# Attention with the scores turned round: keys on the partitions, queries along the free dimension

## The chip, the cores and the metric

The kernel runs on one core of a Trainium2 chip. The metric is the device time of one execution in microseconds (us). TensorE (PE) multiplies, VectorE (DVE) and ScalarE (ACT) work element by element, GpSimd (POOL) does small vector work, and SyncE (SP) issues the transfers.

## The reference

A two-layer trunk: a gated linear recurrence (HGRN2), then multi-head latent attention (MLA), for 1024 latent tokens that see 256 context tokens. The change is in the attention of the second layer: 16 heads, 1024 queries, 1280 keys.

```python
def _attend(q_nope, q_pe, k_nope, k_pe, v):
    s = (jnp.einsum('bqhd,bkhd->bhqk', q_nope, k_nope, preferred_element_type=jnp.float32)
         + jnp.einsum('bqhr,bkr->bhqk', q_pe, k_pe, preferred_element_type=jnp.float32))
    p = jax.nn.softmax(s * MLA_SCALE, axis=-1)
    return jnp.einsum('bhqk,bkhd->bqhd', p.astype(v.dtype), v)
```

## The kernel before

Everything is float32. A product that needs float32 precision is made of three float32r products (`mm3`): each operand is split into a high part, which ScalarE rounds, and a low part, which VectorE subtracts (`split`: `hi` and `lo`, in the tiles `wh`/`wl`, `ph`/`pl`, `oh`/`ol`).

The keys are not expanded per head. `attn_prep` folds a head's key weight into its queries (`qah`, `qal`, in buffers of the tags `wl` and `wh`), so all heads share one latent key matrix (`kh`, `kl`, 128 by 1280), one rope matrix `kr` and one value matrix (`vh`, `vl`, ten tiles of 128 keys). A head's own value weight (`wvh`, `wvl`) is applied behind the average.

The work goes in tiles of 128 queries, 8 to a head, 128 in all. Below, a *unit* is two tiles (256 queries of one head); there are 64 units.

- `attn_scores`, for one tile: queries on the partitions, keys along the free dimension, in blocks of 512, 512 and 256. Five products a block (lines 855 to 859) fill a PSUM tile `s`, of which there are four. VectorE reduces each block to a maximum per query (line 861) and the three to one (867). ScalarE takes the exponential with that maximum as bias and gives the sum of the row (871). VectorE divides the 128 by 1280 probabilities `pr` by the sum (877, 878, 882).
- `attn_values`, for a unit: TensorE transposes the probabilities, 20 blocks of 128 by 128 (902), into PSUM tiles `pt`. ScalarE and VectorE split each pair of key tiles out of PSUM (907, recorded at 214 and 215) into `ph` and `pl`, and 30 products sum the values in `pv` (915). The average is split (920 to 922, the low part on GpSimd), multiplied by the head's value weight (925), by the gate `z` (927), and stored.
- `attend` sorts the steps of these generators by a due time; TensorE keeps this order, while the other engines are ordered by the scheduler. `attn_prep` of the next head runs in between. Behind the last unit the first eight steps of the output projection (`lead`, called `tail` in `attend`) are mixed in.

Of the kernel before, what the change touches and what calls it, by code (L numbers as in the profile page):

```python
# [18 lines left out]
P = 128  # L19
# [18 lines left out]
class Net:  # L38
# [631 lines left out]
    def mla_in(self, pool, pp, kp, a, hh, hl, st):  # L670
# [6 lines left out]
        for c in range(NT):  # L677
# [39 lines left out]
            )  # L717
            if lat:
# [64 lines left out]
    def attn_prep(self, pool, pp, a, st, qrD, zT, h, box):  # L783
# [4 lines left out]
        z = t(pool, [P, LQ], F32, f"za{h % 2}")  # L788
        nc.sync.dma_start(z, zT[h])
# [7 lines left out]
        self.split(wvh, wvl, wv)  # L797
        ps = t(pp, [P, 512], F32, G_TAG)
# [6 lines left out]
        self.split(wqh, wql, ps[:, : 2 * P].rearrange("p (a b) -> p a b", a=2), SCALE)  # L805
        yield
        if h % 2 == 0:
            par = h // 2 % 2
            if ("low", par) not in box:
                box["low", par] = [t(pool, [P, LQ], F32R, f"qrl{par}") for _ in range(2)]  # L810
                for rl in box["low", par]:
                    nc.vector.memset(v32(rl[64:]), 0.0)
            box["pair"] = [(t(pool, [P, LQ], F32R, f"qrh{par}"), rl) for rl in box["low", par]]
            for b, n in self.qgs:
                sl = slice(b * P, (b + n) * P)
                ps = t(pp, [P, 512], F32, G_TAG)
                for j in range(n):
                    nc.tensor.transpose(ps[:, j * P : (j + 1) * P], qr[:, b + j], self.ident)
                for i, (rh, rl) in enumerate(box["pair"]):
                    own, twin = (slice(0, 64), slice(64, P))[:: 1 - 2 * i]  # L820
                    src = ps[own, : n * P]
                    nc.scalar.activation(rh[own, sl], src, AF.Copy, scale=SCALE)
                    nc.vector.scalar_tensor_tensor(
                        rl[:64, sl], src, SCALE, v32(rh[own, sl]), ALU.mult, ALU.subtract
                    )
                    TWIN(nc)(rh[twin, sl], rh[own, sl])
                yield
        qah = t(self.wpool, [P, LQ], F32R, "wl")
        qal = t(self.wpool, [P, LQ], F32R, "wh")
        for b, n in self.qgs:  # L830
            sl = slice(b * P, (b + n) * P)
            ps = t(pp, [P, 512], F32, G_TAG)
            for k in range(2):
                self.mm3(ps[:, : n * P], wqh[:, k], wql[:, k], st["qh"][:, k, sl], st["ql"][:, k, sl], k == 0, k == 1)
            self.split(qah[:, sl], qal[:, sl], ps[:, : n * P])
            yield
        box[h] = (qah, qal) + box["pair"][h % 2] + (wvh, wvl, z)

    def attn_scores(self, pool, pp, st, box, i, prs):
        nc, t, NT = self.nc, self.t, self.NT  # L840
        mm = nc.tensor.matmul
        LK = NT * P
        blocks = [(o, min(512, LK - o)) for o in range(0, LK, 512)]
        nb = len(blocks)
        h, j = divmod(i, self.NL)
        qah, qal, rh, rl = box[h][:4]
        js = slice(j * P, (j + 1) * P)
        mx = t(pool, [P, 4], F32, "mx")
        sm = t(pool, [P, 4], F32, "sm")
        pr = t(pool, [P, LK], F32, "pr")  # L850
        sc = []
        for b, (o, w) in enumerate(blocks):
            s = t(pp, [P, 512], F32, "s")
            ks = slice(o, o + w)
            mm(s[:, :w], qah[:, js], st["kh"][:, ks], start=True, stop=False)  # L855
            mm(s[:, :w], qah[:, js], st["kl"][:, ks], start=False, stop=False)  # L856
            mm(s[:, :w], qal[:, js], st["kh"][:, ks], start=False, stop=False)  # L857
            mm(s[:, :w], rh[:, js], st["kr"][:, ks], start=False, stop=False)  # L858
            mm(s[:, :w], rl[:, js], st["kr"][:, ks], start=False, stop=True)  # L859
            with self.tc.high_priority(offset=AT_PRIO):  # L860
                nc.vector.tensor_reduce(mx[:, b : b + 1], s[:, :w], AX.X, ALU.min)  # L861
            sc.append(s)
            if b < nb - 1:
                yield
        nm = t(pool, [P, 1], F32, "nm")
        with self.tc.high_priority(offset=AT_PRIO):
            nc.vector.tensor_reduce(nm, mx[:, :nb], AX.X, ALU.min)  # L867
        for b, (o, w) in enumerate(blocks):
            yield
            with self.tc.high_priority(offset=EXP_PRIO):  # L870
                nc.scalar.activation(  # L871
                    pr[:, o : o + w], sc[b][:, :w], AF.Exp, bias=nm, scale=-1.0,
                    accum_out=sm[:, b : b + 1],
                )
        yield
        rs = t(pool, [P, 1], F32, "rs")
        nc.vector.tensor_reduce(rs, sm[:, :nb], AX.X, ALU.add)
        nc.vector.reciprocal(rs, rs)
        if i % NORM_ACT[1] < NORM_ACT[0]:
            nc.scalar.activation(pr, pr, AF.Copy, scale=rs)  # L880
        else:
            nc.vector.tensor_scalar(pr, pr, rs, None, ALU.mult)
        prs[i] = pr

    def attn_values(self, pool, pp, st, box, u, prs, yT):
        nc, t, NT = self.nc, self.t, self.NT
        tiles = [i for i in (2 * u, 2 * u + 1) if i < self.NH * self.NL]
        h, b = divmod(tiles[0], self.NL)
        n = len(tiles)
        N = n * P  # L890
        wvh, wvl, z = box[h][4:]
        np_ = -(-NT // 2)
        parts = {}
        acc = None
        for e in range(np_ + PV_LAG):
            if e < np_:
                m = min(2, NT - 2 * e)
                tp = t(pp, [P, 2, 2 * P], F32, "pt")
                for c in range(m):
                    for j, i in enumerate(tiles):  # L900
                        k = 2 * e + c
                        nc.tensor.transpose(  # L902
                            tp[:, c, j * P : (j + 1) * P], prs[i][:, k * P : (k + 1) * P], self.ident
                        )
                ph = t(pool, [P, 2, 2 * P], F32R, "ph")
                pl = t(pool, [P, 2, 2 * P], F32R, "pl")
                self.split(ph[:, :m, :N], pl[:, :m, :N], tp[:, :m, :N])
                parts[e] = (m, ph, pl)
            if e >= PV_LAG:
                if acc is None:  # L910
                    acc = self.pv[:, u % 2]
                m, ph, pl = parts.pop(e - PV_LAG)
                for c in range(m):
                    k = 2 * (e - PV_LAG) + c
                    self.mm3(acc[:, :N], st["vh"][:, k], st["vl"][:, k], ph[:, c, :N], pl[:, c, :N], k == 0, k == NT - 1)
            yield
        oh = t(pool, [P, 2 * P], F32R, "oh")
        ol = t(pool, [P, 2 * P], F32R, "ol")
        o32 = t(pool, [P, 2 * P], F32, "o32")
        nc.scalar.copy(o32[:, :N], acc[:, :N])  # L920
        nc.scalar.copy(oh[:, :N], o32[:, :N])
# [3 lines left out]
        self.mm3(ps[:, :N], wvh, wvl, oh[:, :N], ol[:, :N], True, True)  # L925
        y = t(pool, [P, 2 * P], F32, "ya")
        nc.vector.tensor_tensor(y[:, :N], ps[:, :N], z[:, b * P : b * P + N], ALU.mult)
        nc.sync.dma_start(yT[h][:, b * P : b * P + N], y[:, :N])

    def attend(self, pool, pp, a, st, qrD, zT, yT, box, tail):  # L930
        NL, NH = self.NL, self.NH
        n = NH * NL
        self.pv = self.t(pp, [P, 2, 2 * P], F32, "pv")
        prs = {}
        steps = []
        for h in range(1, NH):
# [454 lines left out]
```

## Time and profile before

| | |
|---|---|
| median of 3 runs | 3146.5 us (3145.36 to 3148.09) |
| the profiled execution | 3146.84 us, of which the span is 3145.1 us |
| TensorE busy | 3108.3 us, 99% of the span |
| VectorE busy | 2164.4 us, 69% |
| ScalarE busy | 1729.6 us, 55% |
| GpSimd busy | 188.3 us, 6% |
| granted TensorE clock | 0.995 of full |

The span is the time between the first and the last instruction; the 1.7 us that the execution takes longer lie around it. A matmul's record includes the time in which it drains, beside the next one, so a busy TensorE says that it always had something to do; what one matmul costs in a row of them is the step from start to start. The records of VectorE and ScalarE overlap a little in the same way. The attention begins near 2131 us and ends, with the `lead` steps, near 2990 us.

### The profile page before, as it was taken

The page shows a single profiled execution, that of the slowest core. Times are in us where ns is not written, and L with a number is a line of the kernel's source. Part 1 is how long each engine was busy: PE and PEld are TensorE (multiplying, and loading weights), DVE is VectorE, ACT ScalarE, POOL GpSimd, SP SyncE. Part 2 cuts the span into 40 slices and gives each one's busy share as a digit, 9 for nine tenths or more (in the row PEclk, how much of TensorE's full clock was granted, in tenths as well). Part 3 has the DMA queues.
Part 4 walks back from the last instruction along what each step waited for, and adds up shares of the span by engine and source line. Part 5 has one row for each costly group of instructions (what it writes and reads, how often), then busy time and mean ns, then how long its engine had stood idle before and what let it go on. Part 6 is the DMA issues. An engine that isn't in the chain of part 4 may idle for free.

```text
span 3145.1 us, 51475 instructions
## 1 busy us (share of the span) xinstructions
PE 3108.3 (99%) x19412; PEld 2782.5 (88%) x19412; DVE 2164.4 (69%) x4898; ACT 1729.6 (55%) x4263; POOL 188.3 (6%) x305
## 2 busy tenths in 40 slices
PE   8899999999999999999999999999999999999999
PEld 7889989899898998988988888788999999999887
DVE  7777688776886758757585563536777777777642
ACT  6556465564655646655475563224666666666532
POOL 0000000000000000000000011000010000000000
PEclk8999999999999999999999999999999999999999
DMA  5110212102111021010127661430101011101261
GB/s 212 43 56 23 74 36 63 56 23 75 36 56 57 24 73 36 30 40 25 41 69 243 222 197 45 141 117 24 41 30 38 24 34 34 34 28 38 69 219 57
DMA packets 100009, 218.88 MB, mean 70 GB/s; under 512 B 10289, under 2 KB 47409, under 8 KB 99761
## 3 DMA queue, kind: packets, MB, share of 16 engines
q1 hardware_dynamic: 99760, 215.59, 21.1%
q8 instruction: 153, 2.51, 0.3%
q14 instruction: 96, 0.78, 0.1%
HBM read 175.70 MB, written 39.85 MB: 69 GB/s over the span
## 4 chain that ended last, share of the span: by engine, by line
PE 92%; DVE 3%; issue 2%; DMA 2%; ACT 1%; POOL 0%; SPq 0%; DVEq 0%; POOLq 0%; ACTq 0%
PE g L265 12%; PE g L264 12%; PE g L263 12%; PE lv L335 6%; PE pt L902 4%; PE o L486 3%; PE pv L263 2%; PE s L855 2%; PE pv L264 2%; PE pv L265 2%; PE s L856 2%; PE s L858 2%; PE s L859 2%; PE s L857 2%; PE lv L263 2%; PE lv L265 2%
## 5 line engine op out<-in xcount | busy, mean ns | idle before, releaser
L263 PE MATMUL g<-hh,wh 128*128 128x512 f32 (+1 forms) x1512 | 548.4, 363 | 3.3 <-DVE hh L253 1.6
L265 PE MATMUL g<-hl,wh 128*128 128x512 f32 (+1 forms) x1512 | 542.4, 360 | 3.0 <-DVE hl L254 3.0
L264 PE MATMUL g<-hh,wl 128*128 128x512 f32 (+1 forms) x1512 | 543.3, 359 | 0.0
L263 PEld LDWEIGHTS g<-hh,wh 128*128 128x128 f32 x1512 | 286.5, 189 | 40.6 <-DVE hh L253 2.0
L265 PEld LDWEIGHTS g<-hl,wh 128*128 128x128 f32 x1512 | 285.7, 189 | 39.0 <-DVE hl L254 3.8
L215 DVE TENSOR_TENSOR wl<-raw,wh 128x1024 fp32r<-128x1024 f32 (+1 forms) x170 | 207.7, 1224 | 160.8 <-ACT wh L214 149.4
L264 PEld LDWEIGHTS g<-hh,wl 128*128 128x128 f32 x1512 | 286.4, 189 | 35.9
L861 DVE TENSOR_REDUCE mx<-s 128x1 f32<-128x512 f32 (+1 forms) x384 | 229.7, 599 | 94.5 <-PE s L859 93.0
L871 ACT ACTIVATE pr<-s,nm 128x512 f32<-128x512 f32 (+1 forms) x384 | 232.7, 615 | 99.1 <-DVE nm L867 92.8
L335 PE MATMUL lv<-QX,KX 128*128 128x128 f32 x1920 | 263.1, 275 | 5.8 <-ACT QX L407 4.3
L335 PEld LDWEIGHTS lv<-QX,KX 128*128 128x128 f32 x1920 | 246.6, 192 | 14.8 <-ACT QX L407 5.5
L214 ACT CAST wh<-raw 128x1024 fp32r<-128x1024 f32 (+1 forms) x170 | 178.0, 1049 | 121.8 <-PE lv L264 38.2
L214 ACT CAST ph<-pt 128x512 fp32r<-128x512 f32 x320 | 187.8, 587 | 96.2 <-PE pt L902 86.6
L215 DVE TENSOR_TENSOR pl<-pt,ph 128x512 fp32r<-128x512 f32 x320 | 219.4, 686 | 12.6 <-ACT ph L214 12.5
L263 PE MATMUL g<-wh,hh 128*128 128x256 f32 (+2 forms) x676 | 197.6, 293 | 0.0
L263 PE MATMUL pv<-ph,vh 128*128 128x256 f32 x640 | 196.7, 307 | 0.0
L265 PE MATMUL g<-wl,hh 128*128 128x256 f32 (+2 forms) x676 | 196.4, 291 | 0.0
L902 PE MATMUL pt<-ident,pr 128*128 128x128 f32 x1280 | 192.5, 273 | 0.1
L264 PE MATMUL g<-wh,hl 128*128 128x256 f32 (+1 forms) x654 | 187.9, 287 | 0.0
L407 ACT COPY KX<-K 128x256 f32<-128x256 f32 (+1 forms) x288 | 109.6, 381 | 131.3 <-PE lv L335 71.3
L265 PE MATMUL pv<-pl,vh 128*128 128x256 f32 x640 | 180.2, 282 | 0.0
L264 PE MATMUL pv<-ph,vl 128*128 128x256 f32 x640 | 180.0, 281 | 0.0
(557 smaller groups left out, 7918.3 us busy)
## 6 DMA issues: line engine op xcount, KB each, us to landing
raw<-in_w_o SPq DMA_DIRECT2D x64, 512.0 KB, 3.8
raw<-in_w_qfbz SPq DMA_DIRECT2D x61, 512.0 KB, 3.8
raw<-in_ada_wT SPq DMA_DIRECT2D x32, 512.0 KB, 3.6
raw<-in_w_mo SPq DMA_DIRECT2D x24, 512.0 KB, 3.9
raw<-in_w_v SPq DMA_DIRECT2D x16, 512.0 KB, 3.6
yT<-Z SPq DMA_DIRECT2D x32, 256.0 KB, 2.0
raw<-in_w_z SPq DMA_DIRECT2D x16, 512.0 KB, 4.1
pyr<-yT SPq DMA_DIRECT2D x64, 128.0 KB, 3.7
```

The costliest lines, as they stand in the source:

```text
L214: nc.scalar.copy(hi, src)
L215: (eng or nc.vector).tensor_tensor(lo, src, v32(hi), ALU.subtract)
L263: mm(ps, lh, rh, start=first, stop=False)
L264: mm(ps, ll, rh, start=False, stop=False)
L265: mm(ps, lh, rl, start=False, stop=last)
L335: nc.tensor.matmul(ps[:, sl], lhs[:, sl], rhs[:, sl], start=True, stop=True)
L407: cp(m12(N[:]), m12(Y))
L486: nc.tensor.matmul(o[:, sl], l, r, start=i == 0, stop=i == len(ops) - 1)
L855: mm(s[:, :w], qah[:, js], st["kh"][:, ks], start=True, stop=False)
L861: nc.vector.tensor_reduce(mx[:, b : b + 1], s[:, :w], AX.X, ALU.min)
L871: nc.scalar.activation(pr[:, o : o + w], sc[b][:, :w], AF.Exp, bias=nm, scale=-1.0, accum_out=sm[:, b : b + 1],)
L902: nc.tensor.transpose(tp[:, c, j * P : (j + 1) * P], prs[i][:, k * P : (k + 1) * P], self.ident)
```

## The change

The scores are computed with 128 keys on the partitions and the 256 queries of a unit along the free dimension, so that the probabilities come out as the value product wants them: the 1280 transposes are gone, as are the division of the probabilities and the due times.

- A unit has five PSUM tiles `s` of two key tiles each (four of the tag `s`, one `s5`); four products a key tile, 256 columns each.
- The maximum over the keys now lies across partitions. VectorE keeps a running elementwise maximum `m2` of the five tiles, read from PSUM (877, 875), and folds it to `mf` (885). TensorE transposes `mf` (888), VectorE reduces it to one maximum per query, `mr` (891), TensorE spreads `mr` over the columns (894), and ScalarE writes its negative as row 64 of the low rope part `rl` (`qrl`, 899). A product of the key matrix `k5`, which has ones in row 64, with `rl` adds the last rope term and subtracts the maximum in PSUM (905). Only then ScalarE takes the exponential (908).
- GpSimd adds the five tiles of exponentials (916, 918); VectorE adds the two halves left (`l`, 927); a product with a column of ones gives the sum per query (969). The quotient is taken at the end: the reciprocal goes to DRAM and comes back spread over the partitions (`rb`, 975 and 980), and VectorE multiplies the output by it (982).
- The splits of `p` into `ph` (ScalarE, 938) and `pl` (VectorE, 944), and `ol` (VectorE, 965, GpSimd before), read two SBUF tiles.
- `attend` writes the order of TensorE, VectorE, ScalarE and GpSimd out by hand. The values of a unit follow two units behind its scores, its closing product three units behind. The first four weight tiles of `lead` are split during the last units (1324, 1326). PSUM: four `s`, and one each of `s5`, `pt`, `mt`, `pv`.

```diff
+        for e in range(nb):
+            m = min(2, NT - 2 * e)
+            s = t(pp, [P, 512], F32, "s" if e < 4 else "s5")[:, : 2 * N].rearrange("p (a q) -> p a q", a=2)
+            for c in range(m):
+                ks = slice((2 * e + c) * P, (2 * e + c + 1) * P)
+                o = s[:, c]
+                for i, (l, r) in enumerate(((kh, qah), (kl, qah), (kh, qal), (kr, rh))):
+                    mm(o, l[:, ks], r[:, js], start=c + i == 0, stop=c == m - 1 and i == 3)
...
+                    nc.vector.tensor_tensor(m2[:, :m], m2[:, :m], s[:, :m], ALU.max)
...
+                nc.vector.tensor_tensor(mf, m2[:, 0], m2[:, 1], ALU.max)
...
+            nc.tensor.transpose(mt[:, 0, j * P : (j + 1) * P], mf[:, j * P : (j + 1) * P], self.ident)
...
+            nc.vector.tensor_reduce(mr, mt[:, 0, :N].rearrange("p (j k) -> p j k", k=P), AX.X, ALU.max)
...
+                mt[:, 1, j * P : (j + 1) * P], mr[:, j : j + 1].broadcast_to([P, P]), self.identr,
...
+            nc.scalar.activation(rl[64:65, js], mt[64:65, 1, :N], AF.Copy, scale=-1.0)
...
+                mm(s[:, c], st["k5"][:, ks], rl[:, js], start=False, stop=c == m - 1, skip_group_check=True)
+            p = t(pool, [P, 2, N], F32, "p")
+            with self.tc.high_priority(offset=EXP_PRIO):
+                nc.scalar.activation(p[:, :m], s[:, :m], AF.Exp)
...
+        add = nc.gpsimd.tensor_tensor
...
+            add(l2, whole[0], whole[1], ALU.add)
+            for p in whole[2:]:
+                add(l2, l2, p, ALU.add)
...
-                        nc.tensor.transpose(
-                            tp[:, c, j * P : (j + 1) * P], prs[i][:, k * P : (k + 1) * P], self.ident
-                        )
...
-        nc.gpsimd.tensor_tensor(ol[:, :N], o32[:, :N], v32(oh[:, :N]), ALU.subtract)
+        nc.vector.tensor_tensor(ol, o32, v32(oh), ALU.subtract)
...
-            with tc.manual_schedule(engines=AT_ORDER):
+            with tc.manual_schedule(engines=AT_HAND):
...
-AT_PSUM = {"s": 4, "pt": 3, "pv": 1}
+AT_PSUM = {"pt": 1, "pv": 1, "mt": 1, "s5": 1}
...
+AT_HAND = {mybir.EngineType.PE, mybir.EngineType.DVE, mybir.EngineType.Activation, mybir.EngineType.Pool}
```

How the order of instructions moves is seen at three places of the steady stretch. On TensorE, before, behind a block of scores stand four transposes of probabilities, then six value products:

```order
L859 MATMUL s_24417<-kr_19998,qrl_4028_21650 128x512
L902 MATMUL pt_24424<-ident_60,pr_24031 128x128
L902 MATMUL pt_24424<-ident_60,pr_24114 128x128
L902 MATMUL pt_24424<-ident_60,pr_24031 128x128
L902 MATMUL pt_24424<-ident_60,pr_24114 128x128
L263 MATMUL pv_21866<-ph_24369,vh_19994 128x256
```

On TensorE now, in the second half of a unit, behind 40 score products (871), 18 value products, the two transposes of `mf` (888) and six more value products, stand the sums of the queries, the closing product, the spread maximum, the last six value products and the subtraction:

```order
L969 MATMUL pt_26144<-ones_20007,l_25815 128x1 x2
L263 MATMUL pt_26144<-oh_26024,wvh_24511 128x256
L264 MATMUL pt_26144<-oh_26024,wvl_24512 128x256
L265 MATMUL pt_26144<-ol_26025,wvh_24511 128x256
L894 MATMUL mt_26094<-identr_20005,mr_26119 128x128 x2
L263 MATMUL pv_21884<-ph_25963,vh_19995 128x256
L264 MATMUL pv_21884<-ph_25963,vl_19996 128x256
L265 MATMUL pv_21884<-pl_25964,vh_19995 128x256
L263 MATMUL pv_21884<-ph_25963,vh_19995 128x256
L264 MATMUL pv_21884<-ph_25963,vl_19996 128x256
L265 MATMUL pv_21884<-pl_25964,vh_19995 128x256
L905 MATMUL s_26034<-qrl_4184_22452,k_3754_20000 128x256 x2
```

The four transposes that stood in each of five places of a unit are gone. Between the spread maximum (894) and the subtraction (905), which waits for ScalarE's row of negatives, stand six products; behind the ten subtractions the next unit's scores follow at once.

On VectorE, before, the maxima, the low parts `pl`, and the division of `pr` stand mixed:

```order
L861 TENSOR_REDUCE mx_26590<-s_26593 128x1
L877 TENSOR_REDUCE rs_26615<-sm_26521 128x1
L878 RECIPROCAL rs_26615<-rs_26615 128x1
L882 TENSOR_SCALAR pr_26522<-pr_26522,rs_26615 128x1280
L215 TENSOR_TENSOR pl_26612<-pt_26606,ph_26611 128x512
```

On VectorE now, one unit from its first maximum to the first `pl` behind `mr` (two `qrl` are the preparation of the next pair of heads):

```order
L877 COPY m_4769_25177<-s_25178 128x512
L875 TENSOR_TENSOR m_4769_25177<-m_4769_25177,s_25188 128x512
L875 TENSOR_TENSOR m_4769_25177<-m_4769_25177,s_25209 128x512
L875 TENSOR_TENSOR m_4769_25177<-m_4769_25177,s_25219 128x512
L875 TENSOR_TENSOR m_4769_25177<-m_4769_25177,s_4777_25229 128x512
L885 TENSOR_TENSOR mf_25240<-m_4769_25177 128x256
L965 TENSOR_TENSOR ol_25167<-o_4766_25168,oh_25166 128x256
L831 SCALAR_TENSOR_TENSOR qrl_4184_22452<-pt_25200,qrh_4772_25198 64x512
L831 SCALAR_TENSOR_TENSOR qrl_4185_22453<-pt_25200,qrh_4773_25199 64x512
L891 TENSOR_REDUCE mr_25265<-mt_25239 128x2
L944 TENSOR_TENSOR pl_25268<-p_25143,ph_25267 128x512
```

The division is gone, the maximum is five instructions in a chain, and `ol` and the preparation stand ahead of `mr`. On ScalarE now, the five `ph` of the unit before stand ahead of the row of negatives (899), and the five exponentials behind it:

```order
L843 CAST wl_25540<-pt_25542 128x512
L938 CAST ph_25607<-p_25487 128x512
L938 CAST ph_25610<-p_25491 128x512
L938 CAST ph_25613<-p_25495 128x512
L938 CAST ph_25616<-p_25499 128x512
L938 CAST ph_25619<-p_25503 128x512
L899 ACTIVATE qrl_4033_21669<-mt_25580 1x256
L908 ACTIVATE p_25657<-s_25520 128x512
```

Before, the exponential waited for VectorE's maximum alone (`nm`); now it waits for TensorE, VectorE, TensorE, ScalarE and TensorE in turn.

## Rows read from the trace of the kernel before

**Rows 1.** The page: busy time of each engine over the span.
```profile
PE 3108.3 (99%) x19412; PEld 2782.5 (88%) x19412; DVE 2164.4 (69%) x4898; ACT 1729.6 (55%) x4263; POOL 188.3 (6%) x305
```
**Rows 2.** Busy us by engine in two stretches of the attention: its start, its middle.
```profile
core 0: us, PE busy (x) PEld busy (x) DVE busy (x) ACT busy (x) POOL busy (x), PEclk, DMA share, GB/s
2130.00:2200.00 70.00, 64.89 (x402) 56.92 (x401) 49.22 (x107) 38.26 (x99) 2.21 (x3) 0.98 0.07 23
2200.00:2800.00 600.00, 600.00 (x4093) 549.26 (x4092) 469.51 (x1001) 375.45 (x967) 50.92 (x71) 1.00 0.11 33
```
**Rows 3.** Timeline of TensorE in the attention: start us, duration us, instruction.
```profile
2501.01 0.40 PE L855 MATMUL s<-kh,wl 128*128 128x512 f32 x1
...
2501.95 0.39 PE L859 MATMUL s<-kr,qrl 128*128 128x512 f32 x1
...
2502.53 0.60 PE L902 MATMUL pt<-ident,pr 128*128 128x128 f32 x4
...
2506.01 0.28 PE L855 MATMUL s<-kh,wl 128*128 128x256 f32 x1
...
2506.48 0.28 PE L859 MATMUL s<-kr,qrl 128*128 128x256 f32 x1
```
**Rows 4.** The page's costliest groups: the transposes of probabilities.
```profile
L902 PE MATMUL pt<-ident,pr 128*128 128x128 f32 x1280 | 192.5, 273 | 0.1
```
**Rows 5.** Other products: two timeline rows, and one line's instructions (duration min/median/max ns).
```profile
502.89 1.06 PE L335 MATMUL lv<-QX,KX 128*128 128x128 f32 x8
...
8.96 3.63 PE L163 MATMUL lv<-csil,adap 128*128 128x2 f32 x32
...
L800 PE MATMUL pt<-wk x64: 270/275/275, 2082.9 to 2875.0; 128*128 128x128 f32 x64
```
**Rows 6.** Timeline of VectorE: pairs that follow each other without a wait.
```profile
2205.72 0.42 DVE L927 TENSOR_TENSOR ya<-pt,za 128x256 f32<-128x256 f32 x1
2206.05 0.42 DVE L212 SCALAR_TENSOR_TENSOR wql<-pt,wqh 128x256 fp32r<-128x256 f32 x1
...
2221.45 0.68 DVE L215 TENSOR_TENSOR wh<-pt,wl 128x512 fp32r<-128x512 f32 x1
2222.05 0.68 DVE L215 TENSOR_TENSOR pl<-pt,ph 128x512 fp32r<-128x512 f32 x1
```
**Rows 7.** Groups by line, 2200 to 2800 us: busy us, mean ns, idle before.
```profile
L214 ACT CAST ph<-pt 128x512 fp32r<-128x512 f32 x233 | 136.6, 586 | 69.8 <-PE pt L902 62.2
...
L920 ACT COPY o<-pv 128x256 f32<-128x256 f32 x47 | 17.5, 373 | 55.2 <-PE pv L265 55.2
```
**Rows 8.** Timeline at the attention's start, where TensorE waits: hand-overs between engines.
```profile
2135.57 0.40 PE L859 MATMUL s<-kr,qrl 128*128 128x512 f32 x1
2135.65 0.69 ACT L871 ACTIVATE pr<-s,nm 128x512 f32<-128x512 f32 x1 [2.79 <-DVE nm L867]
2136.01 0.69 DVE L861 TENSOR_REDUCE mx<-s 128x1 f32<-128x512 f32 x1 [0.39 <-PE s L859]
...
2136.48 0.50 PE L855 MATMUL s<-kh,wl 128*128 128x512 f32 x1 [0.51 <-ACT pr L871]
...
2136.82 0.40 PE L856 MATMUL s<-kl,wl 128*128 128x512 f32 x1
```
**Rows 9.** Timeline: GpSimd's subtraction beside two kinds of VectorE work.
```profile
2408.71 0.74 POOL L922 TENSOR_TENSOR ol<-o,oh 128x256 fp32r<-128x256 f32 x1 [11.22 <-DVE mx L861]
2409.15 0.69 DVE L215 TENSOR_TENSOR pl<-pt,ph 128x512 fp32r<-128x512 f32 x1
...
2421.41 0.88 DVE L882 TENSOR_SCALAR pr<-pr,rs 128x1280 f32<-128x1280 f32 x1
...
2421.86 1.02 POOL L922 TENSOR_TENSOR ol<-o,oh 128x256 fp32r<-128x256 f32 x1 [4.59 <-issue]
```
**Rows 10.** The page's transfers: KB each, median us to landing.
```profile
pyr<-yT SPq DMA_DIRECT2D x64, 128.0 KB, 3.7
```

More of the change, by code (lines that the diff above doesn't have):

```diff
@@ L1 @@
 from contextlib import ExitStack
-from itertools import chain
+from itertools import chain, cycle
 import numpy as np
@@ new lines, in attn_scores @@
+        cell["ps"], cell["parts"] = ps, []
+        add = nc.gpsimd.tensor_tensor
+        whole = [p for m, p in ps if m == 2]
+        l2 = whole[0] if whole else None
+        if len(whole) > 1:
+            l2 = t(pool, [P, 2, N], F32, "l2")
+            add(l2, whole[0], whole[1], ALU.add)
+            for p in whole[2:]:
+                add(l2, l2, p, ALU.add)
+        cell["ps"] = ps
+        cell["sum"] = [x[:, c] for x in (l2,) if x is not None for c in range(2)]
+        cell["sum"] += [ps[-1][1][:, 0]] if ps[-1][0] == 1 else []
@@ L923, in attn_values @@
         yield
         ps = t(pp, [P, 512], F32, G_TAG)
[L925 to L928, printed above, removed]
+        for j in range(n):
+            nc.tensor.matmul(
+                ps[:, 2 * P + j : 2 * P + j + 1], cell["l"][:, j * P : (j + 1) * P], self.ones, start=True, stop=True
+            )
@@ L930, in attend @@
+        yield
+        nc.vector.tensor_tensor(y, y, rb, ALU.mult)
+        nc.sync.dma_start(yT[h][:, b * P : b * P + N], y)
     def attend(self, pool, pp, a, st, qrD, zT, yT, box, tail):
         NL, NH = self.NL, self.NH
[L932 removed]
         self.pv = self.t(pp, [P, 2, 2 * P], F32, "pv")
[L934 to L940 removed]
@@ L951, in attend @@
-        steps += [(n + TAIL_AT + TAIL_GAP * k, tail) for k in range(NH)]
-        steps = sorted(enumerate(steps), key=lambda x: (x[1][0], x[0]))
-        for _, (_, g) in steps:
-            next(g, None)
+        units = [(h, b, min(2, NL - b)) for h in range(NH) for b in range(0, NL, 2)]
+        nb = -(-self.NT // 2)
+        per = -(-NL // 2)
+        preps = chain.from_iterable(
+            self.attn_prep(pool, pp, a, st, qrD, zT, h, box) for h in range(1, NH)
+        )
+        cells, vals, rest = {}, {}, {}
@@ L957 @@
+        for x in vals.values():
+            next(x)
+        for _ in tail:
+            pass
+        for x in list(vals.values()) + list(rest.values()):
+            for _ in x or ():
+                pass
 VEC = {}
@@ L1165, in body @@
         }
+        nc.vector.memset(v32(st["k5"][64:]), 0.0)
+        nc.vector.memset(v32(st["k5"][64:65]), 1.0)
+        net.identr = t(kpool, [P, P], F32R, "identr")
+        nc.vector.tensor_copy(net.identr, net.ident)
+        net.ones = t(kpool, [P, 1], F32, "ones")
+        nc.vector.memset(net.ones, 1.0)
         with ExitStack() as c4:
```

311 lines of the change are left out of this document (196 added, 115 removed).

## Prediction

> **What bounds the kernel now.** I read the page's busy times first: TensorE is busy 99% of the span, no other engine above 69% [rows 1]. Busy is not yet bound, so I looked at the attention by stretches: from 2200 to 2800 us TensorE has no idle time at all, VectorE is busy 469.5 of 600 us, ScalarE 375.5, GpSimd 50.9, and the granted clock is 1.00, the level of 2.4 GHz [rows 2]. At the start, 2130 to 2200 us, TensorE lacks 70 − 64.9 = 5.1 us, while the first units have no value products to hide their maxima. So in the attention TensorE's own work sets the time, and I price it by its steps. Five score products of 512 columns go from 2501.01 to 2501.95 in four steps, 0.235 us each; of 256 columns, from 2506.01 to 2506.48, 0.118 us each [rows 3]. Half the columns cost half the step, so narrower score products lose nothing. Four transposes take 0.60 us of which the last is 0.273 [rows 3, 4], a step of 0.109 us.
>
> A unit before, without preparation: scores 20 × 0.235 + 10 × 0.118 = 5.88; transposes 20 × 0.109 = 2.18; value products 30 × 0.118 = 3.54; closing product 3 × 0.118 = 0.35; in all 11.95 us. The preparation of a head, once in four units, has 12 products of 512 columns (2.8 us), and 0.7 us of transposes and weight products on average: 0.9 us a unit, the same before and after.
>
> **The change on TensorE.** *Removed:* 1280 transposes [rows 4] × 0.109 = 139.5 us. *Scores:* 40 products and 10 subtractions of 256 columns, 50 × 0.118 = 5.90 against 5.88: 0.02 × 64 = +1.3 us. *Added, a unit:* two transposes of `mf`, 0.22; two spread products of `mr`, for which the nearest row is 128 columns with a fresh weight tile, (1.06 − 0.27)/7 = 0.112 each [rows 5], 0.22; two products with the column of ones. These are full float32, which the trace counts as two records each: the 32 products of line 800 (two a head) leave 64 [rows 5]. A record with two columns steps by (3.63 − 0.25)/31 = 0.109 us [rows 5], so four records are 0.44. Together 0.88 × 64 = +56.3 us. If a product with ones left one record, 14 us less: that is the lower bound. The net is −139.5 + 1.3 + 56.3 = **−81.9 us**, 1.28 us a unit. A unit now has 10.7 us of TensorE work, 11.6 with preparation.
>
> **Does the work elsewhere fit under 11.6 us?** *VectorE:* a 128 by 512 operation steps by 0.60 us, a 256 one by 0.33, where nothing waits, though their records say 0.68 and 0.42 [rows 6]. A unit has five maxima in a chain (record and hand-over, 0.72 each: 3.6), five `pl` (3.0), `mf`, `mr`, `ol`, `ya`, `l` and the quotient (6 × 0.33 to 0.42: 2.0 to 2.5), a reciprocal (0.16), and of the preparation about 0.8: 9.6 to 10.1 us, 83 to 87%. By the full records throughout it would be 10.4, still below. *ScalarE:* five exponentials of 0.59 (a cast of that size, [rows 7]) to 0.69 (today's, with the row sum, [rows 8]), five `ph` of 0.59, `o32` and `oh` 0.78, the negatives 0.37, preparation about 1.1: 8.1 to 8.7. *GpSimd:* four sums of 128 by 512; today's 128 by 256 takes 0.74 [rows 9], so each between 0.74 and twice that, 3 to 6 us. *The quotient's way through DRAM:* a load of the size of `rb` lands in 3.7 us [rows 10], and two such trips are less than the unit and a half the order leaves. None of these is the bound.
>
> **What waits in turn.** The new danger is the chain from the last score to the next unit's first, since each `s` has one buffer. I lay one unit out with its first score at 0. Hand-overs: TensorE's end at 2135.97 releases VectorE at 2136.01, 0.04 us; ScalarE's end at 2136.34 lets the waiting product step in about 0.25 later (its successor starts at 2136.82, one step of 0.235 behind) [rows 8]. I take 0.25 for each hand-over to TensorE.
> - Last scores: end of issue at 4.72, drained at 4.88; last maximum 4.92 to 5.61; `mf` to 6.06 (0.42); TensorE could transpose at 6.3. It comes there at 4.72 + 18 × 0.118 = 6.84. Slack 0.5.
> - Transposes drained at 7.2; `mr` to 7.65; TensorE may go on at 7.9. It comes there, behind six value products, the ones and the closing product, at 6.84 + 0.22 + 0.71 + 0.44 + 0.35 = 8.56. Slack 0.6; `ol` and two operations of the preparation stand ahead of `mr` on VectorE, 1.6 us from 6.06, so `mr` can slip to 8.1, still in time.
> - Spread drained at 8.95; ScalarE's negatives to 9.36, as 128 by 256 takes 0.373 [rows 7]; the subtraction may start at 9.61. TensorE comes at 8.56 + 0.22 + 0.71 = 9.49. **Late by 0.12.** ScalarE is free by then: exponentials of the unit before until about 2.5, `o32` and `oh` until 3.3, then `ph` and preparation until about 6.5 to 8.6.
> - Subtraction at 9.61, its first pair drained at 10.0, exponential 0.59 to 0.69, hand-over: the next unit's first score may start at 10.9 to 11.0. TensorE comes at 9.61 + 1.18 = 10.79. **Late by 0.1 to 0.2.**
>
> So two waits of 0.1 to 0.2 us a unit replace none, if the hand-over costs 0.25, and none remain if it costs 0.1. Range 0 to 0.3 × 64 = 0 to 19 us; I take 0.12 × 64 = **+8 us**, since behind a wait the weight load in front of a product costs again and behind no wait it doesn't. VectorE starts a unit about half a microsecond late behind the last `l` and quotient, and makes it up, as maxima of 0.72 follow scores that come every 0.95. What is late next if that cover goes is `mf`, and then the transposes.
>
> **Start and end.** The first two units have no value products. The chain above, from 4.72 to the subtraction, is about 3.3 us uncovered; preparation and its own products fill 0.9 in the first and 1.8 in the second: about 4 us lost, and one table load; before it was 5.1 [rows 2]. At the end the eight `lead` steps have the same products, and the first four weights are ready. I put both together at +1, within −2 to +4. The copies to `k5` and the memsets lie under products ahead of the attention; without that cover 10 × 0.3 = 3 us.
>
> **The sum.** 3146.8 (the profiled execution, 0.3 above the median) − 81.9 + 8 + 1 = **3074 us**, 2.3% faster.
>
> **A rule against the row.** GpSimd's subtraction takes 0.74 us beside a VectorE operation that reads PSUM and one SBUF tile, and 1.02 when it starts 0.45 us into one that reads SBUF alone; VectorE's records are then 0.69 and 0.88, no longer than elsewhere [rows 9]. The new maxima read PSUM and one SBUF tile, so by the row neither is hurt; `mf`, `ol`, `pl` and `l` read two SBUF tiles. The Trainium skill says of this in GPSIMD Engine Reference, Specifications, that GpSimd's SBUF interfaces are shared with VectorE, with contention when the VectorE operation uses two ports or has two SBUF inputs. By that rule the second subtraction's longer time is expected, and the trace agrees; the case where VectorE arrives second, behind a running sum, no row here shows.
>
> **The rivals.**
> - *VectorE waits behind GpSimd's sums.* The sums start when the second exponential is done, about 0.5 into the next unit, and end between 3.5 and 7 of it, just where `mf` (5.6) stands. A sum lasts 0.74 to 1.47 us; if `mf` waits for one, 0.5 is slack and up to 1.0 is lost: at half of that 0.5 × 64 = +32, 3106 us; at worst 3138. For it: the sums and `mf` meet if a sum is long. Against: rows 9 show GpSimd giving way, not VectorE. (It is the rule above read the other way round.)
> - *VectorE is the bound.* At 10.4 us and its chain gaps it would need 1.2 us more a unit to pass TensorE's 11.6; only together with the first. Then about 3095 to 3110.
> - *Slower than before: the chain of the maximum is exposed.* Its place is the pair of waits before the subtraction and before the next scores. It decides at 1.28 us of waiting a unit, four times the 0.3 at the upper end above. It would take hand-overs to TensorE of about 0.8 rather than 0.25, or ScalarE reaching the negatives 1.2 us late, behind its `ph`. Twice as much waiting, 2.5 us, would be 3146.8 + 79 = 3226; just beyond the point, 3160. Against: the hand-over in rows 8, and ScalarE's spare 0.5 to 2.6 us.
> - *No gain, since the transposes were hidden.* They would have to lie in TensorE's idle time, and there is none [rows 2].
>
> **Chances.** The forecast as laid out (3054 to 3085) 0.62; waits behind the sums or a VectorE near its limit (3085 to 3125) 0.24; a gain eaten to within 0.2% (about what a measurement can tell from no change) 0.04; slower, by the exposed chain, 0.07; a gain of between 10 and 20 us the remaining 0.03. Faster 0.89, same 0.04, slower 0.07. The range 3054 to 3108 reaches from the lower bound of the ones' products to half of the first rival's worst.
>
> **What would show it.** TensorE's idle time between 2200 and the end of the attention: some 0.1 to 0.3 us a unit, with ScalarE as the releaser, at lines 905 and 871. The four units of a head take 4 × 11.6 to 11.9 us, down from 51.4. VectorE's maxima keep 0.69, GpSimd's sums 0.74 to 1.5. I am wrong if TensorE waits at line 888 or 894 for VectorE, if a product of 256 columns with keys as weights steps by more than 0.118, or if VectorE's busy share passes 95%.

## The result, and the profile after

The changed kernel takes **3108.9 us** (median of 4 runs, 3104.6 to 3110.0) against 3145.9 for the kernel before, run beside it: a ratio of **0.9879, interval 0.9861 to 0.9896**. It is faster by 37 us where 72 were forecast, and 0.9 us above the upper end of the range. The profiled execution, the fastest of the four, took 3104.64 us (span 3102.9): 31 us above the forecast, the median 35.

The stretches that answer to [rows 2], and the end of the attention (columns as there):

```profile
2130.00:2200.00 70.00, 64.83 (x514) 61.99 (x513) 52.70 (x92) 41.65 (x83) 29.20 (x23) 1.00 0.10 31
2200.00:2800.00 600.00, 592.75 (x4879) 582.44 (x4878) 532.81 (x941) 374.57 (x773) 280.42 (x204) 1.00 0.37 45
2840.00:2960.00 120.00, 98.78 (x598) 87.13 (x597) 72.73 (x119) 49.71 (x95) 25.96 (x18) 0.91 0.57 107
```

The start loses 5.2 us, as before. The middle holds 51 units: 592.75/51 = 11.62 us of TensorE work each, and 7.25 us idle in all. The end is new: in 120 us TensorE is idle for 21.2, and the mean granted clock is 0.91, so that at most another 120 × 0.09 = 10.8 us are lost at the lower of its two levels. Together that is up to 32 us, as much as the whole difference to the forecast. The lower level is seen behind waits. TensorE's timeline, behind its wait for `ol`:

```profile
2891.79 0.38 PE L265 MATMUL pt<-ol,wvh 128*128 128x256 f32 x1 [2.46 <-DVE ol L965]
...
2893.36 0.63 PE L264 MATMUL s<-wh,pyl 128*128 128x512 f32 x1
2893.78 0.63 PE L265 MATMUL s<-wl,pyh 128*128 128x512 f32 x1
...
2896.36 0.40 PE L263 MATMUL s<-wh,pyh 128*128 128x512 f32 x1
2896.60 0.40 PE L264 MATMUL s<-wh,pyl 128*128 128x512 f32 x1
```

A product of 512 columns steps by 0.42 us at 2893 and by 0.24 at 2896; the granted clock from 2892.4 to 2895.4 is 0.51, the level of 1.2 GHz. Not every wait ends so: in the kernel no_trip below, 2.65 us of waiting for the same `ol`, up to 2897.7 us, left the granted clock at 1.00.

Whom TensorE waits for (us in total, times, longest), first in 2200 to 2800, then in 2840 to 3000 us:

```profile
PE pt L969 <- DVE qrl L831: 3.6, 6, 0.6
PE mt L888 <- DVE mf L885: 3.4, 6, 0.6
...
PE s L263 <- ACT pyh L214: 6.9, 2, 5.5
PE acc L263 <- ACT pyh L214: 6.1, 1, 6.1
PE mt L888 <- DVE mf L885: 5.3, 3, 1.8
PE pt L265 <- DVE ol L965: 2.5, 1, 2.5
```

In the middle all of it is VectorE, at `mf` and at the preparation of a pair of heads (`qrl`), once in eight units. At the end the two waits for `pyh`, 13.0 us, are the `lead` steps, which wait for transfers; `mf` and `ol`, 7.8 us, are VectorE. What ScalarE and SP's queue waited for at the end, and the transfers (KB each, median us to landing), the first of the end, the others of the middle:

```profile
ACT pyh L214 <- DMA pyr<-yT: 17.3, 4, 8.8
ACT wh L214 <- DMA raw<-in_w_mo: 17.3, 5, 9.3
...
SPq L980 <- DMA lD<-rc: 19.4, 5, 7.0
...
raw<-in_w_mo SPq DMA_DIRECT2D x13, 512.0 KB, 9.6
...
yT<-ya SPq DMA_DIRECT2D x51, 128.0 KB, 6.3
lD<-rc SPq DMA_DIRECT2D x51, 1.0 KB, 8.8
```

The write of 1 KB of reciprocals takes 8.8 us to land. How this reaches TensorE stands in the chain of work that ended last (start us, us):

```profile
2908.28 11.49 DMA raw<-in_w_mo
...
2932.26 9.33 DMA lD<-rc
...
2942.79 8.22 DMA pyr<-yT
```

Ahead of the first long wait for `pyh` a weight takes 11.49 us to land. Ahead of the second, SP's queue stands at the load of `rb` (980) until the write has landed, and the load of `pyr` is issued only behind it.

VectorE's work on two SBUF tiles is late too. The timeline at two places, and the groups of the middle (count, busy us, mean ns):

```profile
2494.87 1.97 POOL L916 TENSOR_TENSOR l<-p,p 128x512 f32<-128x512 f32 x1 [6.23 <-ACT p L908]
2495.26 0.42 DVE L982 TENSOR_TENSOR ya<-ya,rb 128x256 f32<-128x256 f32 x1
...
2506.87 1.44 POOL L916 TENSOR_TENSOR l<-p,p 128x512 f32<-128x512 f32 x1 [5.92 <-ACT p L908]
2507.08 1.51 DVE L982 TENSOR_TENSOR ya<-ya,rb 128x256 f32<-128x256 f32 x1
...
L982 DVE TENSOR_TENSOR ya<-ya,rb 128x256 f32<-128x256 f32 x51 | 63.0, 1236 | 0.0
L918 POOL TENSOR_TENSOR l<-l,p 128x512 f32<-128x512 f32 x153 | 201.5, 1317 | 12.0
L875 DVE TENSOR_TENSOR m<-m,s 128x512 f32<-128x512 f32 x204 | 140.3, 688 | 56.2 <-PE s L871 43.6 <-issue 0.7 <-DVE m L877 0.5
```

At the second place the product of `ya` and `rb` started 0.21 us into a sum and ended 0.28 us behind its end, 1.51 us for work of 0.42. At the first it took 0.42 us, and the sum beside it 1.97. Nothing lies between: in 38 of the middle's 51 units the product takes 1.50 to 1.52 us; in the other 13 it takes 0.41 or 0.42, and there the unit's first sum takes 1.76 to 2.01 instead of 1.39 to 1.55. One of the two waits out the other. The maxima, which read PSUM and one SBUF tile, keep 0.69 us. (ScalarE's `ph` reads one tile, `p`, and not two as said above.)

### The profile page after: what moved, and what is told of

Read it like the earlier page. It is cut to its first block, busy times and chain, and to the rows that moved or that the text cites. A ratio compares the mean times of both kernels' runs of the same rounds, so it can differ in the third digit from the quotient of the medians.

```text
span 3102.9 us, 52895 instructions
## 1 busy us (share of the span) xinstructions
PE 3039.9 (98%) x19924; PEld 2768.9 (89%) x19924; DVE 2192.3 (71%) x4706; ACT 1691.9 (55%) x3921; POOL 476.7 (15%) x469
## 4 chain that ended last, share of the span: by engine, by line
PE 89%; DVE 5%; issue 2%; DMA 1%; ACT 1%; POOL 0%; DVEq 0%; SPq 0%; POOLq 0%; ACTq 0%
PE g L265 12%; PE g L264 12%; PE g L263 12%; PE s L871 9%; PE lv L335 7%; PE o L486 3%; PE lv L264 3%; PE lv L265 3%; PE lv L263 3%; PE s L905 2%; PE pv L263 2%; PE pv L264 2%; PE pv L265 2%; PE o L451 2%; PE lv L372 1%
## 5 line engine op out<-in xcount | busy, mean ns | idle before, releaser
L81 POOL TENSOR_SCALAR rsq_m<-oss 128x4 f32<-128x4 f32 (+1 forms) x48 | 26.3, 547 | 1529.3 <-ACT ojunk L490 1529.3
L918 POOL TENSOR_TENSOR l<-l,p 128x512 f32<-128x512 f32 x192 | 255.2, 1329 | 15.1
L875 DVE TENSOR_TENSOR m<-m,s 128x512 f32<-128x512 f32 x256 | 176.0, 688 | 68.7 <-PE s L871 53.0
L944 DVE TENSOR_TENSOR pl<-p,ph 128x512 fp32r<-128x512 f32 x320 | 202.8, 683 | 1.4 <-ACT ph L938 1.0
L938 ACT CAST ph<-p 128x512 fp32r<-128x512 f32 x320 | 177.4, 620 | 29.8 <-PE pv L264 28.5
L871 PE MATMUL s<-wl,kh 128*128 128x256 f32 x640 | 186.4, 291 | 2.4 <-ACT p L908 2.4
L263 PE MATMUL pv<-ph,vh 128*128 128x256 f32 x640 | 187.5, 293 | 0.0
L908 ACT ACTIVATE p<-s 128x512 f32<-128x512 f32 x320 | 163.6, 609 | 41.1 <-PE s L905 41.0
```

The costliest lines, as they stand in the source:

```text
L263: mm(ps, lh, rh, start=first, stop=False)
L871: mm(o, l[:, ks], r[:, js], start=c + i == 0, stop=c == m - 1 and i == 3)
L875: nc.vector.tensor_tensor(m2[:, :m], m2[:, :m], s[:, :m], ALU.max)
L908: nc.scalar.activation(p[:, :m], s[:, :m], AF.Exp)
L918: add(l2, l2, p, ALU.add)
L938: self.nc.scalar.copy(ph[:, :m], p[:, :m])
```

## The experiments

Three theories of the loss at the end. **A**: the quotient's way through DRAM holds up the loads of the `lead` steps. **B**: VectorE is late behind GpSimd's sums. **C**: the `lead` steps are late by their own weights. Each kernel is the changed one with the edit shown. All medians are of 4 runs; beside each were 4 to 7 runs of the kernel before on the same chip. The gains below are differences of medians from 3108.9. The kernel before had medians from 3145.9 to 3148.4 beside the different runs, so 2 or 3 us of a gain can lie there; the ratios allow for that.

| run | median us (lowest to highest) | ratio to before, interval |
|---|---|---|
| changed kernel | 3108.9 (3104.6 to 3110.0) | 0.9879, 0.9861 to 0.9896 |
| no_trip | 3091.0 (3090.1 to 3092.2) | 0.9816, 0.9799 to 0.9832 |
| trip_pool | 3116.4 (3112.8 to 3117.8) | 0.9895, 0.9881 to 0.9910 |
| row_trip | 3091.9 (3090.3 to 3094.2) | 0.9824, 0.9809 to 0.9839 |
| near4 | 3096.0 (3093.5 to 3097.9) | 0.9832, 0.9817 to 0.9847 |
| no_sums | 3097.7 (3093.1 to 3098.6) | 0.9835, 0.9820 to 0.9850 |
| mul_later | 3101.6 (3100.7 to 3106.2) | 0.9861, 0.9846 to 0.9876 |
| half_sums | 3101.6 (3100.0 to 3103.6) | 0.9860, 0.9844 to 0.9877 |
| wl_later | 3113.6 (3109.1 to 3116.6) | 0.9895, 0.9880 to 0.9910 |
| lead4 | 3103.1 (3100.2 to 3104.7) | 0.9858, 0.9843 to 0.9873 |
| near4_later | 3091.1 (3086.2 to 3092.6) | 0.9822, 0.9807 to 0.9837 |
| near4_mh | 3086.7 (3085.3 to 3089.4) | 0.9808, 0.9793 to 0.9823 |
| near4_mh_w2 | 3086.0 (3084.3 to 3087.6) | 0.9804, 0.9788 to 0.9820 |

### The quotient's way through DRAM

**no_trip**

```diff
-        nc.sync.dma_start(self.lD[u : u + 1, :N].rearrange("o (j p) -> p (o j)", p=P), rc)
...
-        rb = t(pool, [P, N], F32, "rb")
-        nc.sync.dma_start(rb, self.lD[u : u + 1, :N].broadcast_to([P, N]))
+        rb = z[:, b * P : b * P + N]
```

> Left out: the quotient's way through DRAM in all units; in place of the loaded quotient the tile z is multiplied in, so VectorE has the same operations and the output lacks the division. Theory A (the time lost at the end of the attention comes from the quotient's two transfers, which stand in SP's queue ahead of the loads of the lead steps): 20 to 28 us of the idle time between 2840 and 2960 us go, so about 3080 to 3088 us. Theory B (VectorE is late there behind GpSimd's sums): at most 4 us less, since the sums stay. Theory C (the lead steps are late by their own weights, four of which aren't split ahead): at most 8 us less, the waits for raw stay. The units in the middle keep 11.75 us by all three.

17.9 us less (19.8 by the ratios), a little under A's span and far over those of B and C. The end of the attention, then the landings of the end (first) and the middle (second):

```profile
2840.00:2960.00 120.00, 110.10 (x712) 98.22 (x711) 88.20 (x140) 62.10 (x114) 30.56 (x20) 1.00 0.43 139
...
raw<-in_w_mo SPq DMA_DIRECT2D x20, 512.0 KB, 4.2
...
yT<-ya SPq DMA_DIRECT2D x51, 128.0 KB, 1.8
```

Of 21.2 us idle 9.9 are left, the clock stays at 1.00, and the landings are short again. TensorE waits 0.8 us for `pyh` instead of 13.0, though the eight steps and their weights are the same, so theory C is no cause by itself. What is left is mostly VectorE: 5.3 us for `mf`, 2.6 for `ol`. The middle is as it was (593.02 of 600 us).

**trip_pool**: the same two transfers, for the last four units from GpSimd's queue.

```diff
+        dq = nc.gpsimd if u >= self.NH * -(-self.NL // 2) - 4 else nc.sync
+        dq.dma_start(self.lD[u : u + 1, :N].rearrange("o (j p) -> p (o j)", p=P), rc)
...
+        dq.dma_start(rb, self.lD[u : u + 1, :N].broadcast_to([P, N]))
```

> The two transfers of the quotient of the last four units are issued by GpSimd instead of SP; nothing is left out. Theory A in the form that the order in SP's queue is to blame: the loads of the lead steps no longer stand behind them, 15 to 25 us less than 3109. Theory A in the form that the transfers of 4 bytes themselves keep the DMA engines busy: under 5 us less. Theories B and C: under 5 us less.

7.5 us more (5.0 by the ratios, whose intervals overlap). Taking them out of SP's queue gains nothing, so their order there is not the cause by itself. In the chain that ended last no load waits behind the write any more at 2904 us and later, but the loads themselves land later. From GpSimd the write lands in 10.5 us:

```profile
2921.91 12.56 DMA raw<-in_w_mo
...
2948.69 13.48 DMA pyr<-yT
...
lD<-rc POOLq DMA_DIRECT2D x4, 1.0 KB, 10.5
```

The edit changes the issuing engine as well as the order. The next one changes neither.

**row_trip**: both transfers stay in SP's queue, but the first has one piece instead of 256.

```diff
-        nc.sync.dma_start(self.lD[u : u + 1, :N].rearrange("o (j p) -> p (o j)", p=P), rc)
...
+        nc.sync.dma_start(self.lD[u : u + 1, :N], y[0:1, :N])
```

> Changed: instead of the reciprocals, 256 pieces of 4 bytes from 128 partitions, a row of y, one piece of 1 KB from one partition, is written to lD, so the quotient is replaced by other numbers; issue, waits in the queue, the load of rb and the product stay as they are. If the pieces of 4 bytes make the trip dear (DMA share 0.35 in the attention, landings of raw 9.6 us against 4.2 without the trip): most of the 18 us that leaving the trip out gave, 10 to 18 us less than 3109, and a DMA share near 0.12 in the middle. If it is the trip as such, two transfers in turn in SP's queue: 0 to 5 us less.

17.0 us less: nearly all that leaving out the trip gave. The middle and the end of this kernel, and the two places of the chain above:

```profile
2200.00:2800.00 600.00, 592.57 (x4862) 582.21 (x4861) 509.94 (x936) 376.47 (x775) 285.42 (x204) 1.00 0.16 45
...
2840.00:2960.00 120.00, 112.78 (x700) 101.42 (x699) 83.04 (x133) 59.39 (x111) 30.68 (x20) 0.96 0.42 132
...
2913.33 4.51 DMA raw<-in_w_mo
...
2928.41 2.54 DMA lD<-ya
```

The bytes are the same (45 GB/s), the DMA engines' busy share falls from 0.37 to 0.16. So it is the pieces of 4 bytes: in the middle 15862 packets (the pieces that the trace counts) were under 512 bytes, here 2169, some 268 a write. The weight lands in 4.51 us instead of 11.49, the write in 2.54 instead of 9.33. (The pieces and the partitions that they come from, 128 or one, changed together and weren't parted.)

**near4**: in the last four units, the sum with a matrix of ones as weights, which comes out in all partitions.

```diff
+        near = u >= self.NH * -(-self.NL // 2) - 4
+        if near:
+            nc.tensor.matmul(ps[:, 2 * P : 2 * P + N], self.ones.broadcast_to([P, P]), cell["l"], start=True, stop=True)
...
+            nc.vector.reciprocal(r, r)
```

> The last four units make the sum over the keys with a matrix of ones as weights, so that it comes out in all partitions, and take its reciprocal in PSUM; their quotient needs no transfer. Nothing is left out. Theory A, either form: 18 to 28 us less than 3109, as without the trip, less a reciprocal of 256 elements (0.4 us, or several times that) on VectorE in four units. Theories B and C: under 8 us less, perhaps 2 us more by the reciprocals.

12.9 us less, still below A's span. The reciprocal of 256 elements is dear, and from 2889.9 to 2902.4 us VectorE has no gap; at the end of that row stands an `ol` for which TensorE waits 4.9 us:

```profile
2891.10 1.76 DVE L973 RECIPROCAL pt<-pt 128x256 f32<-128x256 f32 x1
...
PE pt L265 <- DVE ol L965: 4.9, 1, 4.9
```

### GpSimd's sums and VectorE

**no_sums**

```diff
-            add(l2, whole[0], whole[1], ALU.add)
-            for p in whole[2:]:
-                add(l2, l2, p, ALU.add)
```

> Left out: GpSimd's four sums a unit; the sum over the keys is then made of the first and the last pair of key tiles alone. Theory B: VectorE's operations on two SBUF tiles fall back to 0.42 us and the time lost at 2840 to 2880 us goes (5 us), and what follows starts earlier: 8 to 25 us less than 3109. Theory A: under 5 us less, all in the stretch from 2840 to 2880 us, since VectorE has slack in the middle and the transfers stay as they are. The units in the middle fall by less than 0.1 us each by both.

11.2 us less. TensorE never waits in the middle:

```profile
2200.00:2800.00 600.00, 600.00 (x4975) 591.48 (x4974) 489.56 (x958) 382.86 (x789) 0.00 (x0) 1.00 0.41 46
```

So all of the middle's 7.25 us idle time comes from the sums, which A has no place for. At the end the waits for `mf` go as well, but TensorE is idle there for about as long as in the changed kernel, 15.1 us of it for `pyh`:

```profile
2840.00:2960.00 120.00, 99.70 (x564) 86.11 (x563) 60.12 (x110) 47.60 (x91) 0.00 (x0) 0.89 0.73 123
```

While the trip is there, leaving out the sums doesn't lift the end.

**mul_later**: the last step of a unit's values runs behind `mr` of the next unit.

```diff
                     if cur:
                         next(cur)
+                    if rest.get(u - 3):
+                        next(rest[u - 3], None)
...
-            for x in (1, 2):
+            for x in (1,) if cur else (1, 2):
```

> VectorE's product of y and the quotient moves from the end of the unit, where GpSimd's sums run, to behind the reduction of the transposed maxima, where they are done; nothing is left out, and GpSimd does the same work. Theory B (VectorE's operation on two SBUF tiles waits for the end of the running sum, and mf is late by that in some units): that product falls from 1.24 us on average to 0.42, TensorE's idle time in 2200 to 2800 us from 7.2 to under 2 us, and its three waits for mf at the end of the attention from 1.8 to about 0.7 us each; 8 to 12 us less than 3109, about 3098. Rival (the idle time in the middle is the two hand-overs that the prediction laid out, 0.12 us a unit): the product gets short, but the idle time and the total stay within 2 us.

7.3 us less by the medians, a little under what B gave; its range overlaps that of the changed kernel. The trace is plain, in the middle:

```profile
L982 DVE TENSOR_TENSOR ya<-ya,rb 128x256 f32<-128x256 f32 x51 | 21.3, 418 | 0.4
...
2200.00:2800.00 600.00, 598.09 (x4937) 589.02 (x4936) 526.58 (x953) 378.52 (x781) 283.98 (x204) 1.00 0.33 46
```

The product takes 0.418 us, the idle time falls from 7.25 to 1.9 us with GpSimd's work unchanged, and no wait for `mf` is left in the middle. At the end two waits for `mf` stay, of 3.5 us together, where I expected three of 0.7. The trip is unchanged here, and yet `yT` lands in 1.8 us in the middle, not 6.3. In the changed kernel a store is issued at 2508.62, while the write of reciprocals issued at 2504.74 is still under way (the load that waits for it follows at 2512.06); here one is issued at 2506.32, ahead of the next write at 2507.61. So the late landing goes with running beside a write of small pieces.

**half_sums**

```diff
-            add(l2, whole[0], whole[1], ALU.add)
+            for c in range(2):
+                add(l2[:, c], whole[0][:, c], whole[1][:, c], ALU.add)
             for p in whole[2:]:
-                add(l2, l2, p, ALU.add)
+                for c in range(2):
+                    add(l2[:, c], l2[:, c], p[:, c], ALU.add)
```

> GpSimd adds in eight pieces of 128 by 256 instead of four of 128 by 512; nothing is left out. If VectorE waits for the end of the one running operation: a piece lasts about 0.74 us, the product of y and the quotient falls from 1.24 to 0.8 to 1.0 us, the idle time in the middle to about half, 3 to 6 us less than 3109. If VectorE and GpSimd merely share the rate while both run: the product stays at 1.24 us or gets longer, since the sums last a little longer in all, and the total is 0 to 5 us more.

7.3 us less, more than I gave it. GpSimd is busy longer in the middle (308 us, not 280), VectorE's product is shorter:

```profile
L920 POOL TENSOR_TENSOR l<-l,p 128x256 f32<-128x256 f32 x306 | 218.0, 747 | 0.0
...
L984 DVE TENSOR_TENSOR ya<-ya,rb 128x256 f32<-128x256 f32 x51 | 44.8, 879 | 0.0
```

VectorE waits for the end of the one running instruction; a shared rate would have made it later. The mean alone would not show it: in lead4 and row_trip, with sums of the old length, the product takes 0.79 and 0.76 us on average, as there only 17 and 16 of 51 products wait. But those that wait still take 1.50 to 1.53 us there, and 0.95 to 0.97 here (43 of 51).

**wl_later**

```diff
                         self.attn_low(done, 2)
+                    if ahead:
+                        next(tail, None)
...
-                    if ahead:
-                        next(tail, None)
```

> The low halves of the four weights split ahead come, in each of the last units, after the first two pl instead of after l, so past the sums; nothing else moves. Theory B (they are stretched by the sums from 1.22 to 2.32 us and make mf late in three units): 1.2 us again, the three waits for mf of 1.8 us fall below 0.8 us, 3 to 5 us less than 3109. Theory A alone (only the quotient's transfers matter there): within 2 us of it.

4.7 us more by the medians (the ranges meet): my expectation fell. The low half is short, and what it pushed back ran into the sums (VectorE's timeline):

```profile
2851.41 1.22 DVE L1326 TENSOR_TENSOR wl<-raw,wh 128x1024 fp32r<-128x1024 f32 x1
...
2852.95 2.99 DVE L944 TENSOR_TENSOR pl<-p,ph 128x512 fp32r<-128x512 f32 x3
2855.86 1.52 DVE L927 TENSOR_TENSOR l<-l 128x256 f32<-128x256 f32 x1
2857.30 1.52 DVE L982 TENSOR_TENSOR ya<-ya,rb 128x256 f32<-128x256 f32 x1
```

Three `pl` take 1.9 us elsewhere; `mf` is now awaited twice for 5.7 us. At neither of the two places did VectorE have room for the low half in such a unit.

### The lead steps, and combinations

**lead4**: `K_LEAD = 4` instead of 8.

> Four lead steps instead of eight, with the four weights split ahead alone; the other products follow after the attention. Nothing is left out. Theory C (the lead steps are late by their own weights, and that holds up the drain's chain): 8 to 12 us less than 3109. Theory A (the transfers hold up every load there): the waits stay, within 5 us. If the four steps are cover for the drain's chain, 4 x 12 products of 512 columns = 11 us of work that fills it, up to 11 us more.

5.8 us less by the medians, between A and C: TensorE's waits for `pyh` shrink from 13.0 to 6.8 us. That is within the scatter of what A allowed; if C has a part, it is the smaller one.

**near4_later**: near4, mul_later and wl_later in one.

> The quotient of the last four units without a transfer, the product of y and the quotient moved past the sums in the others, and the low halves of the four weights past them as well; nothing is left out. If the two causes are separate, their gains add: 13 us (measured for the first alone) and 8 to 12 us, so 3084 to 3088 us. If the second cause is only covered by the first, or the other way round, it stays above 3092 us. If the low halves bring something of their own, about 3081 us.

3091.1, 17.8 us less: the parts without the low halves gave 12.9 + 7.3 = 20.2. Its range (3086.2 to 3092.6) reaches the 3088.7 that this would be, so it isn't shown that the low halves cost something here.

**near4_mh**: near4, mul_later and half_sums in one.

> The quotient of the last four units without a transfer, the product of y and the quotient moved past the sums in the others, and the sums in pieces of 128 by 256; the low halves of the weights stay where the changed kernel has them. Nothing is left out. The two causes added: 13 us for the transfers, 7 to 10 us for the sums (moved product and pieces attack the same 7 us of idle time in the middle, and each some of the waits for mf at the end): 3086 to 3089 us. If moving the low halves was what kept the earlier combination at 3091, it is below that by 3 to 5 us; if not, 3091.

3086.7, as expected if the two causes add. It is below the combination before it by what the expectation gave to the low halves, but the ranges meet, and the pieces' own share can't be told apart. The end of this kernel and TensorE's largest wait in it:

```profile
2840.00:2960.00 120.00, 112.40 (x682) 98.78 (x681) 88.24 (x132) 60.10 (x111) 35.42 (x39) 0.97 0.55 141
...
PE pt L265 <- DVE ol L967: 4.0, 1, 4.0
```

**near4_mh_w2**: the same with `W_LEAD = 2`.

> As the kernel with all three edits, but two weights are split ahead in the last units instead of four. If VectorE is over its time in these units by the low halves (1.2 us each on top of about 10.4 of 11.7): two waits for mf of 0.8 to 1.8 us less, so 2 to 4 us less than that kernel. If the lead steps need the weights split ahead: two steps wait for a weight's landing, halves and hand-over, 3 to 8 us more.

3086.0, not to be told from near4_mh. The waits for `mf` do fall, from 1.5 to 0.4 us. Either is 22 us below the changed kernel with nothing left out.

## Why the prediction was right and wrong

**TensorE's work: right.** Forecast 11.6 us a unit with preparation, measured 11.62. The products with ones were a little cheaper than the 0.44 us worked out:

```profile
2420.26 0.50 PE L969 MATMUL pt<-ones,l 128*128 128x1 f32 x4
2420.62 0.36 PE L263 MATMUL pt<-oh,wvh 128*128 128x256 f32 x1
```

They step by 0.36 us in all, 5 us less over 64 units, within the scatter of the rest.

**The waits, +8: right in size, wrong in place.** 7.25 us in 51 units are 9 in 64. But neither the subtraction (905) nor the next scores (871) wait in the middle. The hand-over I had put at 0.25 us is 0.15 at most: ScalarE's row of negatives ran from 2504.68 for 0.38 us, and the subtraction began at 2505.21, one step behind the product ahead of it (2505.10). So the right size is luck. What waits is `mf` and the preparation, the place of the first rival, and no_sums and mul_later show its mechanism. The rival's price was too high: `mf` is late by 0.6 us in one unit of eight, not by 0.5 in each. A wait at line 888 for VectorE was one of the signs named for being wrong, and it came.

**VectorE: too low.** Forecast 9.6 to 10.1 us a unit, measured 532.81/51 = 10.4. The difference is the sums: the product with `rb` takes 1.24 us on average instead of 0.42, the addition `l` 0.70, and without the sums VectorE is busy 489.56 us in the same stretch (no_sums), about 9.5 a unit. The prediction left open what VectorE does when it arrives second. The Trainium skill says in SBUF — State Buffer, Who interferes with whom, that a VectorE instruction with two SBUF inputs contends with a GpSimd instruction that reads SBUF, that one with at most one SBUF input, outside the 2-port modes, doesn't, and that the shared port pair is an exclusive lock. That whoever issues first has it for the whole instruction stands there for VectorE's 2-port modes. The runs agree, and show it for two SBUF inputs too: 1.51 us behind a sum of 1.44, 0.95 to 0.97 behind a unit's first pieces (0.92 on average, half_sums), the sum late in place of the product in 13 units, and maxima of 0.69 throughout.

**Start: right.** 5.2 us idle, "about 4 and one table load" forecast.

**The step that failed: "Start and end", at the end (+1; up to 32).** It said that "the eight lead steps have the same products, and the first four weights are ready". The products are the same; their loads are not on time. The step before it had priced the quotient's trip by a load of the size of `rb`, 3.7 us [rows 10], and called two of those covered. The trip *is* covered in the middle. But the write lands in 8.8 us, not 3.7, and its 256 pieces keep the DMA engines busy for everyone else: `yT` lands in 6.3 us instead of 1.8, the weights at the end in 9.6 instead of 4.2. Shown by no_trip and row_trip. My first form of theory A, the order in SP's queue, has a place in the chain (loads stand behind the write for 9.33 us), but taking it away alone gained nothing (trip_pool). The Trainium skill has the rule in DMA: Bandwidth & Descriptors, Rules for kernel authors: a last dimension that isn't contiguous becomes one descriptor per element. The packets counted above agree.

**The rest of the end** is VectorE in the last units: the low halves of four weights, 1.22 us each and 2.3 beside the sums, on an engine that has little over 1 us to spare in a unit.

```profile
2872.30 2.32 DVE L1326 TENSOR_TENSOR wl<-raw,wh 128x1024 fp32r<-128x1024 f32 x1
```

With it go 5.3 us of waits for `mf` and 2.5 for `ol`. That the low halves are their cause is argued from these waits and not shown: wl_later moved the load and didn't lift it, and near4_mh_w2, with half of it, has 1.1 us less of the waits for `mf` and no gain that can be told from the scatter.

**The rivals.** The first rival's 3106 us lies near the measured 3109 by luck. The waits behind the sums are there, but in the middle they cost no more than the +8 that the forecast gave to other waits; what it lacked is mostly the trip, 17 to 18 us, which no rival named.

**Open.** near4_mh is still 13 us above the forecast. Its end has 7.6 us idle, 4.0 of it for an `ol` that stands on VectorE behind a reciprocal of 1.75 us and work stretched by the last sums; the granted clock there (0.97) and the middle (4.8 us idle, 6 over all 64 units, less than the forecast's 8) leave the rest unexplained. Whether trip and sums together explain all of the 31 us wasn't tried in one kernel.

## What to carry to other kernels

Price a transfer by its pieces, not by its bytes, and ask what it does to the transfers beside it where these are on the path: what is hidden in the steady stretch can decide the drain. Work given to GpSimd can cost VectorE the rest of a running instruction at an operation on two SBUF tiles, so keep such operations out of the time of the sums, or make the sums short. Before an engine at 89% gets extra work in some units, look at what it has to spare in one of them: here little over 1 us.

## What the runs showed of the hardware that was not expected

- 1 KB in 256 pieces from 128 partitions takes 8.8 us to land from SP's queue in the middle and 10.5 from GpSimd's at the end, and 2.5 us at one place where it is a single piece; 51 writes in pieces in 600 us raise the DMA engines' busy share from 0.16 to 0.37 at the same 45 GB/s.
- A VectorE product on two SBUF tiles beside a GpSimd sum takes 0.42 or 1.51 us and nothing between; where it takes 0.42, the sum takes 1.76 to 2.01 us instead of about 1.4.
- A reciprocal of 128 by 256 in PSUM takes 1.76 us on VectorE, four times a product of that size (0.42); of 128 by 2 it is 0.16.
- A full float32 product with one column steps by 0.36/4 = 0.09 us a record, two records each.
